# Affine part of two layer norms moved from the rows to the transposed rows and the residual

## Chip, cores and metric

One core of a Trainium2 chip runs the whole kernel. The metric is the device time of one execution in microseconds. The kernel before has a median of 3053.77 us over three runs (3049.5 to 3065.22).

## What is computed

A first block (two kinds of attention, a gate) is followed by two layers. Each layer has a mixer, then this (sequence and width are 1024, the feed-forward width is 4096):

```python
h = layer_norm(DN_ALPHA * h + mix, ln_mix_g[layer], ln_mix_b[layer])
h = layer_norm(DN_ALPHA * h + sq_relu_mlp(h, w_ff1[layer], w_ff2[layer]), ln_ffn_g[layer], ln_ffn_b[layer])
# layer_norm(x, g, b) = (x - mean) * rsqrt(var + eps) * g + b,  sq_relu_mlp(h, w1, w2) = square(relu(h @ w1)) @ w2
```

The change concerns the first of these two norms, in both layers. Its output `h` is used twice: as input of the first feed-forward map and as residual behind the second.

## The kernel before

Everything is in fp32, and a product is three matmuls on a high and a low part of each operand (a "split": ScalarE writes the high part, L155, and VectorE or GpSimd the low part, L157). Both feed-forward maps use a seven-product scheme on blocks of 512 (the products are numbered X[1] to X[7]).

**`lin_ln` (L1186)** is the last product of the mixer, then the norm. Eight tiles of 128 rows go through two column halves. In the second half each tile `t` goes through a chain: VectorE adds the residual (L1215), takes the statistics (L1143, L1144) and prepares the variance (L176), GpSimd raises it to -0.5 (L178), and VectorE applies `(z - mean) * g` (L1152) and `z * rs + b` (L1154), each on 128 x 1024, with `g` and `b` spread over all partitions in two pages that `ln_rows` loads (L1133). The result is stored for the residual (L1221, into `dzr`), and `to_T4` (L1171) turns each half of the row with four TensorE transposes (L1176) and one ScalarE copy of 128 x 512 out of PSUM (L1177) into a page `B`. From the pages `B`, VectorE builds differences (`op`, L1243), and splits make the blocks X[1] to X[7].

Four units of the first map (`ff1_unit`, L1279) begin inside `lin_ln`: the products X[1] and X[2] of units 0 to 3 are issued before the other blocks are ready. Each unit loads its weights (L1313, L1292, L1336), forms sums (L1293 to L1296), splits them, squares what comes out (L1310) and stores it (L1359, L1373).

**`ff` (L1450)** runs `ff1` and then the second map in four sweeps `k` of eight steps `j`. A step's operands are fetched two steps ahead (`AHEAD`, `ff2_ops`): four loads (L1408) and four splits on ScalarE and VectorE. The residual tiles `z` are read back from `dzr` (L1484), and `add` (L1475) adds a finished block of 4 tiles x 512 columns to them (L1479): the quarter (rows 0, columns 0) behind step (0,7), three quarters behind steps (1,7) and (2,7), the last behind sweep 3.

**What sets the order.** Each engine works its queue in order. The queues are laid out ahead of time by a planner from the order of the program and estimated durations, so a changed duration can change the order. All loads and stores of these stages are issued by SP, in order: an issue that waits for its page holds the later ones. Data lives in 48 pages of 128 x 1024 that are handed out first in, first out: a page taken is the one that was freed longest ago, and its new writer waits for the last reader of the old content. PSUM banks 2 and 3 take turns for the transposes.

Of the kernel before, what the change touches and what calls it, by code (L numbers as in the profile page):

```python
# [10 lines left out]
F32 = mybir.dt.float32  # L11
F32R = mybir.dt.float32r
I32 = mybir.dt.int32
AF = mybir.ActivationFunctionType
ALU = mybir.AluOpType
AX = mybir.AxisListType
MUL, ADD, SUB = ALU.mult, ALU.add, ALU.subtract
# [15 lines left out]
LN_EPS = 1e-5 * 4.0 ** -0.5  # L33
# [26 lines left out]
class Kern:  # L60
# [135 lines left out]
    def consts(self):  # L196
        nc, cp, i = self.nc, self.cp, self.i
        self.ident = cp.tile([128, 128], F32, name="ident")
        make_identity(nc, self.ident)
        self.ones = cp.tile([128, 128], F32, name="ones")  # L200
        nc.vector.memset(self.ones, 1.0)
        self.inv128 = cp.tile([128, 1], F32, name="inv128")
        nc.scalar.activation(self.inv128, self.ones[:, 0:1], AF.Copy, scale=1.0 / 128)
        self.halfpi = cp.tile([128, 1], F32, name="halfpi")
        nc.vector.memset(self.halfpi, float(np.float32(np.pi / 2)))
        self.nhalf = cp.tile([128, 64], F32, name="nhalf")
        nc.vector.memset(self.nhalf, -0.5)
        self.cols = cp.tile([128, 32], F32, name="cols")
        nc.sync.dma_start(self.cols, i["cols"])
        self.zeros = cp.tile([128, 128], F32, name="zeros")  # L210
        nc.gpsimd.memset(self.zeros, 0.0)
        self.gq8 = cp.tile([128, 2], F32, name="gq8")
        for j in range(2):
            nc.vector.tensor_scalar(self.gq8[:, j:j + 1], self.cols[:, 8 + 2 * j:9 + 2 * j], 0.125, None, MUL)
# [920 lines left out]
        return out  # L1135

    def ln(self, z, gb, eng=None, st=None):

        V = self.nc.vector
        mv, cs = self.sm(2, "mv"), (0,) if st is not None else (0, 1)  # L1140
        st = self.sm(12, "st") if st is None else st
        for c in cs:
            V.bn_stats(st[:, c * 6:c * 6 + 6], z[:, c * 512:(c + 1) * 512])  # L1143
        V.bn_aggr(mv, st.rearrange("p (n s) -> p n s", s=6))  # L1144
        rs = self.rsq(1, mv[:, 1:2], 1.0, LN_EPS)
        self.ln_apply(z, mv, rs, gb, np.s_[:], eng)

    def ln_apply(self, z, mv, rs, gb, cs, eng=None):

# [18 lines left out]
            nc.scalar.activation(h, src, AF.Copy)  # L1168
            nc.vector.tensor_tensor(l, src, h.bitcast(F32), SUB)

    def to_T4(self, src, dst):  # L1171

        nc = self.nc
        tp = self.bank("tr")
        for j in range(4):
            nc.tensor.transpose(tp[:, j * 128:(j + 1) * 128], src[:, j * 128:(j + 1) * 128], self.ident)  # L1176
        nc.scalar.activation(dst, tp.rearrange("p (c k) -> p c k", k=128), AF.Copy)  # L1177

    def split_T(self, src, X, p, pr, eng):

# [5 lines left out]
    def lin_ln(self, xp, wname, res, scale, j):  # L1186

        nc, i = self.nc, self.i  # L1190
        V, G = nc.vector, nc.gpsimd
        nat = lambda ch: [self.wload(i[wname][ch * 4 + k]).view("p (k f) -> p k f", k=2) for k in range(4)]
        ws = nat(0)
        z = [self.pg() for _ in range(8)]
        for t in range(8):
            nc.sync.dma_start(z[t].t, res[:, t, :])
        gb = self.ln_rows(j)
        x = self.tx(xp)
        self.dzr = self.dr([8, 128, 1024])
        X, B = {}, {}  # L1200
        units = deque()
        for ch in range(2):
            ws = ws if ch == 0 else nat(1)
            self.psum(**(dict(g1=[0, 1], tr=[2, 3], P=[4, 5, 0, 1], Q=[6, 7]) if ch else dict(g1=range(8))))
            for t in range(8):
                ps = self.bank("g1")
                hf, sl = t // 4, slice(t % 4 * 128, (t % 4 + 1) * 128)
                for kt in range(8):
                    w = [a[:, kt % 2, :] for a in ws[kt // 2]]
                    xh, xl = (a[:, sl] for a in x(kt, hf))  # L1210
                    self.mm(ps, xh, w[0], kt == 0, False)
                    self.mm(ps, xh, w[1], False, False)
                    self.mm(ps, xl, w[0], False, kt == 7)
                zs = z[t].t[:, ch * 512:(ch + 1) * 512]
                V.scalar_tensor_tensor(zs, ps, scale, zs, MUL, ADD)  # L1215
                if ch == 1:
                    if t % 4 == 3:
                        self.fr(*xp[0][hf], *xp[1][hf])
                    self.ln(z[t].t, gb)
                    self.dump(f"h{j}", [(np.s_[t::8, :], z[t].t)])  # L1220
                    nc.sync.dma_start(self.dzr[t], z[t].t)  # L1221
                    pr = t % 4 // 2
                    for K in range(2):
                        if t % 2 == 0:
                            B[K, hf, pr] = self.pg((128, 4, 256))
                        self.to_T4(z[t].t[:, K * 512:(K + 1) * 512], B[K, hf, pr].t[:, :, t % 2 * 128:(t % 2 + 1) * 128])
                    self.fr(z[t])
                    if hf == 0 and t % 2:
                        for K in range(2):
                            self.split_T(B[K, 0, pr].t, X, 1 + K, pr, V)  # L1230
                    if t in (4, 6):
                        units.append(self.ff1_unit(j, t // 2 - 2, X, True))
                        next(units[-1])
            self.fr(*(p for w in ws for p in w.pg))
        self.fr(*gb)
        b11, b12, b21, b22 = ([B[K, hf, pr] for pr in range(2)] for K in range(2) for hf in range(2))
        t2 = [self.pg((128, 4, 256)) for _ in range(2)]

        def op(p, o, x, y):

            for pr in range(2):
                if y is not None:
                    V.tensor_tensor(o[pr].t, x[pr].t, y[pr].t, SUB)  # L1243
            for pr in range(2):
                if p:
                    self.split_T(o[pr].t, X, p, pr, V)

        def first(k):

            for _ in range(2):  # L1250
                next(units[k])

        op(0, b11, b12, b11)
        op(6, t2, b22, b11)
        first(0)
        first(1)
        op(7, b12, b22, b12)
        self.fr(*b12)
        for k in (2, 3):
            units.append(self.ff1_unit(j, k, X, True))  # L1260
            next(units[k])
            first(k)
        next(units[0])
        op(5, b11, None, None)
        self.fr(*b11)
        op(4, b21, b21, t2)
        self.fr(*b21, *t2)
        op(3, b22, None, None)
        self.fr(*b22)
        return X, units  # L1270
# [179 lines left out]
    def ff(self, X, units, layer, last):  # L1450


        nc, i = self.nc, self.i
        V, A, G = nc.vector, nc.scalar, nc.gpsimd
        self.ff1(X, units, layer)
        z = [self.pg() for _ in range(8)]
# [5 lines left out]
        def fetch():  # L1462
            if steps:
                ahead.append(self.ff2_ops(layer, *steps.pop(0)))
# [17 lines left out]
            fetch()  # L1482
        for t in range(8):
            nc.sync.dma_start(z[t].t, self.dzr[t])  # L1484
        for k in range(3):
            for j in range(8):
                ops = ahead.popleft()
                fetch()
                if k == 1 and j == 0 and not last:
                    self.mla_tables()  # L1490
                for c, op in enumerate(ops):
                    for t in range(4):
                        mms(c, op, t, j == 0 and (k == 0 or k == 1 and c == 1), j == 7)
                    self.fr(*op[0], *op[1])
                    if j == 7:
                        for r, h in (((0, 0),), ((0, 1),), ((1, 1),))[k] if c == 0 else (((0, 0),), ((1, 1),), ((0, 1),))[k]:
                            add(c, r, h)

        gb = self.ln_rows(2 + layer)
# [33 lines left out]
        st = [self.sm(12, "sth") for _ in range(4)]  # L1533
        for t in range(4):
            V.bn_stats(st[t][:, 6:12], z[4 + t].t[:, 512:])
        if last:
            for t in range(4):
                for n, op in enumerate(tail):
                    mms(0, op, t, False, n == 3)
                zs = z[4 + t].t[:, :512]  # L1540
# [304 lines left out]
def layout(v):  # L1845
    o = {}
    f32 = np.float32
    v = {k: np.asarray(a) for k, a in v.items()}
# [4 lines left out]
        o["w_" + n] = w[:, :, c].reshape(4, 2, 128, 512).transpose(0, 2, 1, 3).reshape(4, 128, 1024)  # L1853
    wz = v["w_in"][0].reshape(8, 128, 8, 4, 128)[:, :, [3, 7]]
    o["w_z"] = wz.transpose(2, 3, 1, 0, 4).reshape(8, 128, 1024)
    cols = np.zeros((128, 32), f32)
    cols[:, 0:8] = v["norm_g"][0].reshape(8, 128).T
    for j, n in ((8, "q_norm_a"), (9, "k_norm_a"), (10, "q_norm_b"), (11, "k_norm_b")):
        cols[:, j] = np.tile(v[n][0], 2)
# [1 line left out]
    o["cols"] = cols  # L1861
    cols[:, 13:15] = v["kv_norm_g_2"].reshape(2, 128).T
    cols[:, 15:18] = v["q_norm_g_2"][0].reshape(3, 128).T
    o["lamv"] = np.broadcast_to(np.stack([v[n][0] for n in ("lam_q1", "lam_k1", "lam_q2", "lam_k2")])[None], (128, 4, 64))
    p_, j_ = np.arange(128)[:, None], np.arange(1920)[None]
    rel = j_ - 896 - p_
    n = np.abs(rel)
# [7 lines left out]
    c = cb * 16 + qc  # L1875
# [5 lines left out]
    for row in range(16):  # L1881
        rb, qr = row // 8, row % 8
        rs = min(max(row - 4, 0), 8)
# [8 lines left out]
    pr = lambda a: a.reshape(32, 2, 64, -1).transpose(1, 2, 0, 3).reshape(128, 32, -1)  # L1892
# [47 lines left out]
```

## Time and profile before

| | us |
|---|---|
| median of 3 runs | 3053.77 |
| profiled execution | 3052.07 |
| its span in the trace | 3050.3 |
| granted clock over the span | 0.982 |

The profile is of one execution; times inside it count from the start of its span. The engines are PE (TensorE), PEld (its weight loads), DVE (VectorE), ACT (ScalarE), POOL (GpSimd) and SP (which issues DMAs); a q behind a name is the engine's queue. In rows, `p` is a page, `ps` PSUM, `dr` a buffer in DRAM, `in_...` an input, and `out<-in` says what is written from what. The granted clock is given as a share of full speed. In the stage of layer 0 the tiles go through the norm from 1262 to 1323 us, in layer 1 from 2360 to 2421 us; the second map runs from 1637 and from 2730 us.

### The profile page before, as it was taken

How to read it: one execution, taken by the hardware profiler on the slowest of the kernel's cores; microseconds unless marked ns; L12 is line 12 of the kernel's file. 1: busy time of each engine (PE TensorE's matmuls, PEld its weight loads, DVE VectorE, ACT ScalarE, POOL GpSimd, SP SyncE). 2: the span in 40 equal slices, each digit the busy share in tenths (PEclk: the TensorE clock that was granted, in tenths of full speed). 3: DMA queues.
4: the chain of work that ended last, by engine and by line, in shares of the span. 5: the costliest groups of instructions: out<-in, count | busy, mean ns of one | idle time of the engine just before them, and what ended most of it. 6: DMA issues, size and time to landing. Idle time of an engine off the chain costs nothing.

```text
span 3050.3 us, 38397 instructions
## 1 busy us (share of the span) xinstructions
PE 2917.8 (96%) x14380; PEld 2403.1 (79%) x14380; DVE 1879.5 (62%) x2754; ACT 1188.6 (39%) x1810; POOL 1053.8 (35%) x694
## 2 busy tenths in 40 slices
PE   7999889998999899989999999999999999999998
PEld 6777667776777788867887888988898778878887
DVE  8555547765359700486667875655553966667666
ACT  4333237775324322142224433345563432334331
POOL 5545527754522333234441002112353244420001
PEclk9999999999999999999999999999999999999999
DMA  4353463368545113134448877311123334479673
GB/s 163 131 177 115 124 199 104 93 193 249 192 158 166 42 56 128 59 123 150 152 150 317 295 252 251 110 44 48 34 75 125 121 131 152 152 268 340 237 273 134
DMA packets 240923, 479.04 MB, mean 157 GB/s; under 512 B 26816, under 2 KB 76224, under 8 KB 240736
## 3 DMA queue, kind: packets, MB, share of 16 engines
q1 hardware_dynamic: 240592, 476.45, 46.2%
q8 instruction: 113, 1.85, 0.3%
q14 instruction: 74, 0.61, 0.1%
q10 hardware_dynamic: 144, 0.13, 0.0%
HBM read 320.00 MB, written 148.11 MB: 153 GB/s over the span
## 4 chain that ended last, share of the span: by engine, by line
PE 55%; DVE 10%; DMA 5%; issue 3%; POOL 2%; ACT 1%; SPq 0%; DVEq 0%; POOLq 0%; ACTq 0%
PE ps L170 23%; PE ps L1471 19%; PE ps L1276 10%; DMA p<-in_w_ff 3%; POOL p L157 1%; DMA p<-dr 1%; PE ps L1753 1%; DVE p L1030 1%; DVE p L157 1%; DVE p L1310 1%; DVE p L1043 1%; ACT p L155 1%; DMA dr<-p 1%; DVE p L1154 0%; DVE p L1036 0%
## 5 line engine op out<-in xcount | busy, mean ns | idle before, releaser
L170 PE MATMUL ps<-p,p 128*128 128x512 f32 (+6 forms) x7448 | 1532.1, 365 | 62.9 <-POOL p L157 11.7
L170 PEld LDWEIGHTS ps<-p,p 128*128 128x128 f32 (+2 forms) x7448 | 1214.5, 185 | 311.4 <-issue 50.3
L157 POOL TENSOR_TENSOR p<-p,p 128x1024 fp32r<-128x1024 f32 (+2 forms) x272 | 604.5, 2235 | 946.5 <-ACT p L155 861.2
L155 ACT ACTIVATE p<-p 128x1024 fp32r<-128x1024 f32 (+2 forms) x558 | 520.9, 959 | 959.0 <-DMA p<-in_w_ff 160.3
L1276 PE MATMUL ps<-p,p 128*128 128x512 f32 x2688 | 631.8, 396 | 31.8 <-ACT p L155 12.4
L1276 PEld LDWEIGHTS ps<-p,p 128*128 128x128 f32 x2688 | 509.2, 191 | 151.8 <-ACT p L155 14.7
L1471 PE MATMUL ps<-p,p 128*128 128x512 f32 x2688 | 613.0, 390 | 3.4 <-DVE p L1479 1.6
L1471 PEld LDWEIGHTS ps<-p,p 128*128 128x128 f32 x2688 | 503.6, 188 | 110.6 <-issue 2.4
L157 DVE TENSOR_TENSOR p<-p,p 128x1024 fp32r<-128x1024 f32 (+1 forms) x286 | 315.4, 1129 | 109.7 <-ACT p L155 108.6
L178 POOL TENSOR_TENSOR rsd<-rst,nhalf 128x1 f32<-128x1 f32 (+1 forms) x64 | 104.8, 1639 | 534.9 <-DVE rst L176 533.1
L1310 DVE SCALAR_TENSOR_TENSOR p<-p 128x512 f32<-128x512 f32 x96 | 116.6, 1214 | 2.2
L1122 DVE SCALAR_TENSOR_TENSOR p<-p,ps 128x1024 f32<-128x1024 f32 x8 | 9.8, 1221 | 141.4 <-ACT p L1121 141.4
L496 DVE CUSTOM_DVE_ANT_0 p<-ps,bw 128x1024 f32<-128x1024 f32 x64 | 77.3, 1219 | 30.7 <-PE ps L170 21.2
L498 ACT ACTIVATE p<-p,m 128x1024 f32<-128x1024 f32 x64 | 73.4, 1149 | 31.6 <-DVE m L496 19.6
L1295 DVE TENSOR_TENSOR p<-p,p 128x512 f32<-128x512 f32 x32 | 34.8, 1088 | 75.0 <-DMA p<-in_w_ff 75.0
L511 POOL TENSOR_TENSOR p<-p,p 128x1024 f32<-128x1024 f32 x32 | 76.8, 2405 | 2.0
L1747 POOL TENSOR_SCALAR p<-p,rz 128x256 f32<-128x256 f32 (+6 forms) x64 | 48.7, 762 | 68.7 <-DVE rz L1746 67.2
L1757 DVE TENSOR_TENSOR p<-ps,p 128x512 fp32r<-128x512 f32 (+3 forms) x96 | 50.9, 553 | 33.0 <-ACT p L1756 32.3
L1177 ACT ACTIVATE p<-ps 128x512 f32<-128x512 f32 x32 | 17.5, 594 | 129.5 <-PE ps L1176 129.4
L157 DVE TENSOR_TENSOR p<-ps,p 128x1024 fp32r<-128x1024 f32 (+1 forms) x42 | 42.0, 1015 | 39.9 <-ACT p L155 37.2
L510 POOL TENSOR_SCALAR p<-p,c 128x1024 f32<-128x1024 f32 x32 | 37.1, 1158 | 85.0 <-DVE c L509 62.1
L663 POOL TENSOR_SCALAR p<-p,rz 128x384 f32<-128x384 f32 x64 | 38.1, 601 | 68.3 <-DVE rz L662 53.3
(266 smaller groups left out, 2569.8 us busy)
## 6 DMA issues: line engine op xcount, KB each, us to landing
p<-dr SPq DMA_DIRECT2D x254, 512.0 KB
p<-in_w_ff SPq DMA_DIRECT2D x184, 512.0 KB
dr<-p SPq DMA_DIRECT2D x126, 512.0 KB
dr<-p SPq DMA_DIRECT2D x248, 256.0 KB
bw<-in_rpbw SPq DMA_DIRECT2D x16, 768.0 KB
dr<-p SPq DMA_DIRECT2D x80, 128.0 KB
p<-p SPq DMA_DIRECT2D x64, 128.0 KB
p<-dr SPq DMA_DIRECT2D x32, 256.0 KB
```

The source lines that it names most:

```text
L155: nc.scalar.activation(hi, src, AF.Copy, scale=scale)
L157: (eng or nc.gpsimd).tensor_tensor(lo, src, hi.bitcast(F32), SUB)
L170: self.nc.tensor.matmul(out, l, r, start=start, stop=stop)
L178: nc.gpsimd.tensor_tensor(dst, t, self.nhalf[:, :n], ALU.pow)
L496: V.tensor_tensor_reduce(out=s.t, in0=ps, in1=bw[:, 896 - 128 * t:1920 - 128 * t], scale=-1.0, scalar=3e38, op0=ADD, op1=ALU.min, accum_ou ...
L498: A.activation(s.t, s.t, AF.Exp, bias=m[:, c:c + 1], scale=-1.0, accum_out=z[:, c:c + 1])
L511: G.tensor_tensor(p[0].t, p[0].t, p[1].t, ADD)
L1276: self.nc.tensor.matmul(ps, w[a][:, kt, :], x[b][kt // 2].t[:, kt % 2, :], start=start and kt == 0 and (a, b) == (0, 0), stop=kt == 3 and ...
L1310: V.scalar_tensor_tensor(h, h, 0.0, h, ALU.max, MUL)
L1471: nc.tensor.matmul(ps[c][t], a[x].t[:, kt, t * 128:(t + 1) * 128], b[y].t[:, kt, :], start=start and kt == 0 and (x, y) == (0, 0), stop=st ...
L1747: G.tensor_scalar(s.t[:, :n], s.t[:, :n], rz, 1.0, MUL, MUL)
L1757: V.tensor_tensor(atl[kq][:, :nb, qi * 128:(qi + 1) * 128], tv, oh.bitcast(F32), SUB)
```

## The change

The norm in `lin_ln` now only makes `(z - mean) * rs`, in one VectorE instruction on 128 x 1024. This is what is stored in `dzr` and transposed. After the transposition a feature is a partition, so `g` and `b` are one value per partition; four ScalarE instructions of 128 x 128 with a scale and a bias per partition replace the one copy of 128 x 512 per half row. `g` and `b` for this lie in 32 further columns of the constant `cols`. The residual gets its scale and bias in `ff`: `ln_rows` is called there behind the residual's loads, its two pages live until step (1,5), and VectorE multiplies and adds each quarter of `z` in steps (0,3), (1,1), (1,3) and (1,5), 8 instructions of 128 x 512 each time.

```diff
-        self.cols = cp.tile([128, 32], F32, name="cols")
+        self.cols = cp.tile([128, 64], F32, name="cols")
...
     def ln(self, z, gb, eng=None, st=None):
+        mv, rs = self.ln_stats(z, st)
+        self.ln_apply(z, mv, rs, gb, np.s_[:], eng)
+
+    def ln_stats(self, z, st=None):
...
-        rs = self.rsq(1, mv[:, 1:2], 1.0, LN_EPS)
-        self.ln_apply(z, mv, rs, gb, np.s_[:], eng)
+        return mv, self.rsq(1, mv[:, 1:2], 1.0, LN_EPS)
...
-    def to_T4(self, src, dst):
+    def to_T4(self, src, dst, gb):
...
-        nc.scalar.activation(dst, tp.rearrange("p (c k) -> p c k", k=128), AF.Copy)
+        for j in range(4):
+            nc.scalar.activation(dst[:, j], tp[:, j * 128:(j + 1) * 128], AF.Identity, bias=gb[:, 1, j:j + 1], scale=gb[:, 0, j:j + 1])
...
-        gb = self.ln_rows(j)
+        gb = self.cols[:, 32 + 16 * j:48 + 16 * j].rearrange("p (c k) -> p c k", c=2)
...
-                    self.ln(z[t].t, gb)
-                    self.dump(f"h{j}", [(np.s_[t::8, :], z[t].t)])
+                    mv, rs = self.ln_stats(z[t].t)
+                    V.tensor_scalar(z[t].t, z[t].t, mv[:, 0:1], rs, SUB, MUL)
...
-        self.fr(*gb)
...
         for t in range(8):
             nc.sync.dma_start(z[t].t, self.dzr[t])
+        gz = self.ln_rows(layer)
+
+        def affine(r, h):
+
+            c = slice(h * 512, (h + 1) * 512)
+            for t in range(4):
+                zs = z[4 * r + t].t[:, c]
+                V.tensor_tensor(zs, zs, gz[0].t[:, c], MUL)
+                V.tensor_tensor(zs, zs, gz[1].t[:, c], ADD)
+
...
+                if (k, j) in ((0, 3), (1, 1), (1, 3), (1, 5)):
+                    affine(*((0, 0), (0, 1), (1, 1), (1, 0))[0 if k == 0 else 1 + j // 2])
+                if (k, j) == (1, 5):
+                    self.fr(*gz)
```

## Rows read from the trace of the kernel before

**Rows 1.** Busy time, share of the span, instructions (the page, part 1)

```profile
PE 2917.8 (96%) x14380; PEld 2403.1 (79%) x14380; DVE 1879.5 (62%) x2754; ACT 1188.6 (39%) x1810; POOL 1053.8 (35%) x694
```

**Rows 2.** Busy us by stretch: PE, PEld, DVE, ACT, POOL, clock, DMA share

```profile
1270.00:1335.00 65.00, 57.11 (x275) 46.11 (x274) 59.73 (x76) 26.91 (x45) 21.53 (x12) 0.95 0.38 134
1335.00:1340.00 5.00, 5.00 (x15) 3.95 (x14) 5.00 (x7) 2.89 (x6) 0.00 (x0) 0.59 0.00 0
1365.00:1370.00 5.00, 5.00 (x24) 4.14 (x23) 2.49 (x4) 1.72 (x3) 3.14 (x2) 1.00 0.84 295
2430.00:2435.00 5.00, 3.84 (x8) 2.75 (x9) 4.92 (x6) 3.54 (x7) 0.00 (x0) 0.50 0.14 54
2435.00:2440.00 5.00, 5.00 (x17) 3.91 (x17) 5.00 (x8) 2.00 (x4) 0.00 (x0) 0.68 0.01 3
```

**Rows 3.** Waits of PE: 1150 to 1345 us, then 2310 to 2480 (total us, times, longest)

```profile
PE ps L1276 <- ACT p L155: 6.4, 2, 4.1
PE ps L1276 <- DVE p L157: 1.2, 2, 0.9
PE ps L1276 <- DVE p L1330: 0.3, 1, 0.3
...
PE ps L1276 <- ACT p L155: 5.8, 2, 3.5
PE ps L1276 <- DVE p L157: 1.4, 2, 1.2
```

**Rows 4.** Timeline of layer 0: start, us, engine, instruction [idle before <-releaser]

```profile
1290.98 1.28 DVE L1152 SCALAR_TENSOR_TENSOR p<-p,mv,p 128x1024 f32<-128x1024 f32 x1
1291.20 1.46 POOL L178 TENSOR_TENSOR rsd<-rst,nhalf 128x1 f32<-128x1 f32 x1 [1.53 <-DVE rst L176]
1292.70 1.28 DVE L1154 SCALAR_TENSOR_TENSOR p<-p,rsd,p 128x1024 f32<-128x1024 f32 x1 [0.45 <-POOL rsd L178]
```

**Rows 5.** By line and form: count, busy us, mean ns, idle before

```profile
L1154 DVE SCALAR_TENSOR_TENSOR p<-p,rsd,p 128x1024 f32<-128x1024 f32 x31 | 39.3, 1276 | 5.3 <-POOL rsd L178 5.3
...
L1294 DVE TENSOR_TENSOR p<-p,p 128x512 f32<-128x512 f32 x32 | 21.8, 680 | 12.0 <-DMA p<-in_w_ff 12.0
...
L864 DVE TENSOR_SCALAR p<-p 128x1024 f32<-128x1024 f32 x4 | 2.8, 691 | 0.1
...
L376 ACT ACTIVATE p<-ps,rx 128x512 f32<-128x512 f32 x40 | 27.4, 685 | 82.6 <-PE ps L170 82.6
...
L1177 ACT ACTIVATE p<-ps 128x512 f32<-128x512 f32 x32 | 17.5, 594 | 129.5 <-PE ps L1176 129.4
...
L350 ACT ACT_TABLE_LOAD x4 | 5.1, 1283 | 0.1
...
L1756 ACT ACTIVATE p<-ps 128x128 fp32r<-128x128 f32 x16 | 4.4, 277 | 0.5 <-PE ps L1753 0.4
```

**Rows 6.** Timeline at the end of the stage of layer 0

```profile
1325.54 1.06 ACT L155 ACTIVATE p<-p 128x1024 fp32r<-128x1024 f32 x1 [0.51 <-DMA dr<-p]
...
1326.65 1.49 PE L1276 MATMUL ps<-p,p 128*128 128x512 f32 x4 [2.31 <-ACT p L155]
```

**Rows 7.** Waits of ScalarE, 1282 to 1346 us

```profile
ACT p L155 <- DVE p L1243: 7.8, 3, 4.9
```

**Rows 8.** Chain of waits, stage of layer 1

```profile
2424.96 5.09 DMA p<-in_w_ff
```

**Rows 9.** Second map of layer 0, by stretch (columns as in rows 2)

```profile
1645.00:1650.00 5.00, 5.00 (x24) 4.14 (x23) 5.00 (x7) 2.96 (x4) 0.00 (x0) 1.00 1.05 402
1700.00:1750.00 50.00, 50.00 (x222) 41.40 (x221) 44.09 (x50) 18.79 (x19) 0.00 (x0) 1.00 0.83 292
```

**Rows 10.** Timeline of VectorE in the second map of layer 0

```profile
1777.50 1.21 DVE L1438 TENSOR_TENSOR p<-p,p 128x1024 f32<-128x1024 f32 x1
...
1814.16 0.68 DVE L1479 SCALAR_TENSOR_TENSOR p<-ps,p 128x512 f32<-128x512 f32 x1
```

**Rows 11.** Timeline of PE, second map of layer 1

```profile
2745.16 35.12 PE L1471 MATMUL ps<-p,p 128*128 128x512 f32 x152 [0.77 <-ACT p L155]
```

## What the change will do to the time: the prediction

> **What bounds the kernel now.** I read the page first. TensorE is busy for 96% of the span, VectorE for 62% [rows 1]: what the change can give must come out of the few places where TensorE stands still, and only if VectorE is what it waits for there. So next I read the stretches around the changed norm. In 1270 to 1335 us VectorE is busy for 59.73 of 65 us and TensorE for 57.11, while ScalarE has 26.91 [rows 2]: this is one of the places where VectorE is the full engine. The waits of TensorE price it. In the stage of layer 0 it waits 6.4 + 1.2 + 0.3 = 7.9 us, in layer 1 5.8 + 1.4 = 7.2 us [rows 3], and nearly all of it falls behind the last tile, when VectorE has to finish norm, differences and splits at once. Those waits cost more than themselves: right behind them the granted clock is 0.59 in layer 0 and 0.50 (the lower of its two levels, 1.2 GHz) and 0.68 in layer 1, and 15, 8 and 17 matmuls pass in 5 us where a stretch at clock 1.00 has 24 [rows 2]. At 5/24 = 0.21 us each, layer 0 loses 9 x 0.21 = 1.9 us. Layer 1 has 25 matmuls in 10 us, of which 1.16 were waiting: 8.84/0.21 = 42, so 17 are missing, 3.6 us. All that the stage can give back is therefore 7.9 + 7.2 + 1.9 + 3.6 = 20.6 us, 0.7% of the time.
>
> **The sum's base.** The profiled execution took 3052.07 us (span 3050.3, 1.8 around it), 1.7 under the median of 3053.77. The three runs shown lie 0.5% apart, which is about what a measurement of this kernel can tell from no change: 15.3 us, so under 3038.5 counts as faster and over 3069.0 as slower.
>
> **Norm on VectorE.** Each tile loses two instructions of 1.28 us [rows 4, 5] and gains one with a single tensor source. The trace has no such instruction with two values per partition. Its nearest row is the 128x1024 TENSOR_SCALAR at 691 ns, and the upper bound is the 1276 ns of the one it replaces [rows 5]. I take 0.69, the same shape and operation: 2 x 1.276 - 0.69 = 1.86 us less VectorE work a tile, 14.9 us a layer.
>
> How much of this reaches TensorE is the main choice. The first three tiles pass while TensorE has products to do, so only tiles 3 to 7 count. In the old order GpSimd's power (1.46 us) runs beside the first of the two instructions (1.28 us), and the second waited 0.45 us for it [rows 4]. The new instruction needs mean and power both, so VectorE has nothing of this tile to do in those 1.46 us. The tile's own chain from the start of the power shrinks only from 1293.98 - 1291.20 = 2.78 us to 1.46 + 0.04 + 0.69 = 2.2 us, by 0.6 us. Lower bound per layer: 0.6 us for the tiles before and the full 1.86 us for the last, whose instructions stand in a stretch without idle time: 2.5 us. Upper bound: five tiles at 1.86 = 9.3 us, cut to the 7.9 and 7.2 us that there are. I take the last tile in full and half of tiles 4 to 6, on the view that splits or statistics of other tiles are put into every second gap: 1.86 + 0.5 x 3 x 1.86 = 4.65 us a layer, **-9.3 us**. What is late next is the difference for X[7] (L1243) and the lower part of unit 3's weights.
>
> **Clock.** TensorE will still wait some 3 us a layer, and the clock fell behind waits of 2.3 and 4.1 us [rows 3, 6]. Bounds 0 and 5.5 us; I take 1 us a layer, **-2 us**.
>
> **ScalarE.** A 128x128 copy out of PSUM takes 277 ns, and a value per partition adds 685 - 594 = 91 ns [rows 5]. A piece with scale and bias is then 277 + 182 = 459 ns, four of them 1.84 us against 0.594, at most 1.25 us more a half row, 2.5 us a tile, 20 us a layer. ScalarE has that room (26.91 + 20 of 65 us). On the path it costs only where a split stands behind these pieces. In that stretch ScalarE waits 7.8 us for VectorE's differences [rows 7], which covers most of the 3 x 2.5 = 7.5 us of tiles 5 to 7; if the cover were gone, 7.5 us a layer. Against it, the split at 1325.54 waited for a store of the last tile, whose page it was to fill, and TensorE 2.31 us for that split [rows 6]. The norm no longer takes two pages here, every later writer gets a page freed two places earlier, and this one goes to a page that TensorE has left. I take +0.5 us a layer, **+1 us**.
>
> Identity occurs nowhere in the trace. If it asked for a table load of 1.28 us [rows 5] before and after, twice a layer, that is at most 5.1 us; I take 0 and leave the bound to the range. The Trainium skill ("ScalarE: Activation LUTs", section "Table sets: the hidden batching unit") says that cheap functions, identity among them, are part of every set, so that no load would come; no run here shows it, and by it the sum stays as it is.
>
> **Second map, VectorE.** Four quarters of 8 instructions of 0.68 us [rows 5] are 21.8 us a layer. They lie in sweeps 0 and 1, where TensorE has no gap to speak of and VectorE is busy for up to 44.09 of 50 us [rows 9]. The cover is the distance by which it works ahead: it starts on sweep 2 (L1438) at 1777.50, while the first block of sweep 1 is added only at 1814.16, 36.7 us later [rows 10]. The 3 x 5.4 = 16.3 us in sweep 1 leave 20 us of it. Cost 0; without that cover each quarter would cost up to 5.4 us.
>
> **Second map, loads.** `ln_rows` leaves SP's queue ahead of the norm, where TensorE is not waiting, and its two issues and two pages come between the residual's loads and those of step 2. They are 2 x 0.52 MB in the stretch where the DMA engines are full, 402 GB/s at share 1.05 [rows 9]: 1.05 MB / 402 GB/s = 2.6 us for the loads queued behind, those of steps 2 and 3. Step 1 had no slack (TensorE waited 0.77 us in it [rows 11]); from then on the distance grows by some us a step. Bounds: 0 if step 1's loads go first, as the order of the program has it, and 2.6 us if the rows go first. I take 0.7 us a layer, **+1.4 us**. If an issue waits for its page, SP holds the fetches behind it, and step 2 is late next. The transposes, the store into `dzr` and the 32 more columns of a constant change nothing that I can price.
>
> **Sum.** -9.3 - 2 + 1 + 1.4 = -8.9 us: 3052.07 - 8.9 = **3043.2 us**.
>
> **Rivals.**
> *The whole wait goes (20%).* The order of VectorE's queue is planned anew, and if it fills every gap behind a power, the stage's upper bound holds: 20.6 us less, 1.4 us for the loads back, 3032.9 us. For it: VectorE is the full engine of the stage [rows 2]. Against it: the difference for the last tile still needs power, transposes and eight ScalarE pieces in a row.
> *The loads decide (12%).* In layer 1 the chain runs through a weight load of 5.09 us [rows 8] whose issue stands behind a store on SP. If the next wait is for such loads, VectorE idles instead and the stage gives about 1 us a layer, less 0.7: 3051.5 us. This is the case in which the change does not do what it says.
> *ScalarE is late (10%), slower than before.* If the planner leaves the splits behind the pieces of tiles 5 to 7, each layer pays 7.5 us and gets only the lower bound of 2.5 us back: 2 x 5 = 10 us, 3062 us. It decides from the point where the pieces in front of the last splits exceed the 7.8 us that ScalarE waits there now [rows 7]; 7.5 is just under it, which speaks for and against. The Trainium skill ("ScalarE: Activation LUTs", section "Rules for kernel authors") gives multiply and add to VectorE and not to ScalarE; by that rule this rival is how it goes. In busy time the trace agrees, with up to 2.5 us added a tile against 1.86 taken away.
>
> **Chances and range.** My case has 58%, and its own bounds run from 3036 (gain 7.5 a layer, loads free) to 3052 (lower bound of the gain, 2.6 us a layer for the loads, no clock). Faster by over 0.5% is most of the first rival and the quick end of my case: 0.28. Slower by over 0.5% needs the third rival together with full costs of loads and tables (3062 + 2.6 x 2 + 5.1): 0.07. The rest, 0.65, is within 0.5%. The range 3030 to 3060 leaves out the far end of the first rival and most of the third.
>
> **What would show it.** Right: in the norm one TENSOR_SCALAR of about 0.7 us a tile, idle before it put down to the power, TensorE's waits in the two stages down from 7.9 and 7.2 us to about 3, those around a clock of 0.5 shorter, and no longer wait in the second map. Wrong: new waits of TensorE for ScalarE's Identity pieces or splits, the new instruction near 1.3 us, a wait in step 1 or 2 of the second map grown by over 1 us, or a table load in the stage. A change of several us in the stages between, through other pages and orders, would also make the total wrong without touching these steps.

## The result, and the profile after

The changed kernel takes 3078.66 us, median of 5 runs (3076.87 to 3080.91); the kernel before, on the same chip, 3056.32 (3049.5 to 3065.22). The ratio is 1.0073, 95% interval 1.0058 to 1.0088: **slower by 0.7%**, outside the predicted range, on the side that had been given a chance of 7%. The profiled executions have spans of 3050.3 and 3076.3 us, 26.0 apart.

Where they went is read from the starts of fixed matmuls in the two traces (the lines of the matmuls are now L1280 for the first map, L1475 for the second). The first row of the table runs from a fixed matmul ahead of the norm to the 169th matmul of the first map, the second from there to the first matmul of the second map; both together are "norm and first map" further down:

| us | before, layer 0 / 1 | after, layer 0 / 1 | difference of both |
|---|---|---|---|
| norm, up to the 169th matmul of the first map | 130.8 / 138.0 | 128.1 / 133.9 | -6.8 |
| rest of the first map | 278.3 / 273.9 | 275.7 / 276.3 | -0.1 |
| second map, sweep 0 (384 matmuls) | 91.1 / 91.2 | 106.7 / 106.8 | **+31.2** |
| everything else | | | +1.7 |

The last line holds +2.9 us in the first 1230 us, whose instructions the change does not touch; over the programs below that part lay between -3.0 and +9.4 us of before. The kernels are therefore compared stage by stage.

The first part of the page (busy time, share of the span, instructions) hardly shows a change against [rows 1]:

```profile
PE 2924.6 (95%) x14380; PEld 2410.7 (78%) x14380; DVE 1872.6 (61%) x2802; ACT 1220.1 (40%) x1906; POOL 1056.2 (34%) x694
```

By line and form (count, busy us, mean ns, idle before), the new instructions and the table loads:

```profile
L1181 ACT ACTIVATE p<-ps,cols 128x128 f32<-128x128 f32 x128 | 47.6, 464 | 112.3 <-PE ps L1179 112.2
...
L350 ACT ACT_TABLE_LOAD x4 | 5.1, 1283 | 0.1
...
L1224 DVE TENSOR_SCALAR p<-p,mv,rsd 128x1024 f32<-128x1024 f32 x16 | 13.0, 810 | 4.2 <-POOL rsd L178 3.8
```

The prices are near those of the prediction: 464 ns a piece (459 foreseen), 810 ns for the norm's one instruction (690 taken, 0.12 us a tile too little), and still only the four table loads of [rows 5]. So the places decide, not the prices. TensorE's waits (total us, times, longest) in the norm of layer 0 (1150 to 1345 us), the norm of layer 1 (2330 to 2480), and the second map of layer 0 (1640 to 2000); the last line is the only one of that last stretch in the kernel before:

```profile
PE ps L1280 <- ACT p L155: 3.3, 2, 2.3
PE ps L1280 <- DVE p L157: 2.2, 1, 2.2
PE ps L1280 <- DVE p L1334: 0.6, 1, 0.6
...
PE ps L1280 <- ACT p L155: 4.6, 3, 2.3
PE ps L1280 <- DVE p L157: 2.2, 1, 2.2
PE ps L1280 <- DVE p L1334: 1.6, 1, 1.6
...
PE ps L1475 <- ACT p L155: 7.1, 1, 7.1
PE ps L1475 <- DVE p L157: 5.4, 1, 5.4
...
PE ps L1471 <- DVE p L157: 1.0, 1, 1.0
```

In the norm 7.9 us became 6.1 in layer 0 [rows 3]. In layer 1 they did not fall: they are 8.4 us, and were 8.1 up to the 169th matmul (the 7.2 us of the prediction are the two largest lines of that view). What layer 1 gained, 4.1 us, came with the clock, as the windows from the fixed matmul to the 169th show, first before, then after (total, PE, PEld, DVE, ACT, POOL, granted clock, DMA share, GB/s):

```profile
2318.77:2456.76 137.99, 129.79 (x592) 105.78 (x590) 96.16 (x125) 42.96 (x69) 40.04 (x19) 0.95 0.30 103
...
2333.59:2467.50 133.91, 125.58 (x585) 102.78 (x583) 80.38 (x117) 57.20 (x117) 39.67 (x19) 0.97 0.31 110
```

How far that carries, the six kernels below whose norm is that of the changed kernel show. Up to the 169th matmul they take 127.0 to 128.2 us in layer 0 and 134.4 to 138.3 in layer 1: there the changed kernel's 133.9 is the shortest, and rows_only and late_rows, with a clock of 0.95, gain nothing. So layer 0's 2.7 us stand, and layer 1's 4.1 us lie inside what the same instructions vary by.

The new thing stands in the two lines of L1475: 12.5 us in a place where TensorE had waited 1.0. The timeline of that place (start, us, engine, instruction, count), first TensorE, then VectorE, then SP's queue:

```profile
1638.26 10.13 PE L1475 MATMUL ps<-p,p 128*128 128x512 f32 x44
1655.53 4.92 PE L1475 MATMUL ps<-p,p 128*128 128x512 f32 x12 [7.14 <-ACT p L155]
1665.87 34.35 PE L1475 MATMUL ps<-p,p 128*128 128x512 f32 x142 [5.42 <-DVE p L157]
...
1639.79 2.35 DVE L157 TENSOR_TENSOR p<-p,p 128x1024 fp32r<-128x1024 f32 x2
1642.06 0.68 DVE L1372 TENSOR_TENSOR p<-p,p 128x512 f32<-128x512 f32 x1
1642.66 7.30 DVE L1496 TENSOR_TENSOR p<-p,p 128x512 f32<-128x512 f32 x12
...
1661.59 0.68 DVE L1375 TENSOR_TENSOR p<-p,p 128x512 f32<-128x512 f32 x1
1662.19 2.49 DVE L1497 TENSOR_TENSOR p<-p,p 128x512 f32<-128x512 f32 x4
...
1680.17 0.68 DVE L1497 TENSOR_TENSOR p<-p,p 128x512 f32<-128x512 f32 x1
...
1632.11 0.33 SPq L1133 DMA_DIRECT2D p<-in_ln  x1
...
1636.01 0.34 SPq L1133 DMA_DIRECT2D p<-in_ln  x1
1637.28 0.37 SPq L1412 DMA_DIRECT2D p<-in_w_ff  x1
...
1651.73 10.88 SPq L1377 DMA_DIRECT2D dr<-p  x3
1662.72 2.02 SPq L1412 DMA_DIRECT2D p<-dr  x2
```

L1496 and L1497 are the multiplies and adds of the residual. The program has them at steps (0,3), (1,1), (1,3) and (1,5); VectorE's queue has **all 32 in one clump** between 1642.66 and 1680.85 us, from the first step on, and the splits (L157) of the next steps between them and behind them. The loads of the two rows (L1133) went out before a weight load (L1412) of the first steps. And a store (L1377) whose values VectorE makes in L1372 to L1375 sits at the head of SP's queue: VectorE reaches L1375 only at 1661.59, the three stores take from 1651.73 to 1662.61, and every load behind them waits. The windows of this stretch (columns as above) show the rest of the price:

```profile
1650.00:1655.00 5.00, 0.00 (x0) 0.00 (x0) 5.00 (x7) 1.52 (x2) 0.00 (x0) 0.78 1.06 399
1655.00:1660.00 5.00, 4.47 (x11) 3.55 (x12) 5.00 (x8) 2.37 (x3) 0.00 (x0) 0.54 0.51 199
1660.00:1665.00 5.00, 0.45 (x2) 0.01 (x1) 5.00 (x8) 2.00 (x2) 0.00 (x0) 0.80 0.36 118
1665.00:1670.00 5.00, 4.13 (x10) 3.26 (x11) 5.00 (x6) 2.01 (x2) 0.00 (x0) 0.51 0.75 251
1670.00:1675.00 5.00, 5.00 (x24) 4.11 (x23) 5.00 (x7) 0.10 (x1) 0.00 (x0) 1.00 0.01 3
```

In the stretch VectorE has not one idle moment, the DMA engines fall from share 1.06 to 0.36 although weights are wanted, and behind each wait the granted clock is near 0.5, the 1.2 GHz level, so that 11 and 10 matmuls pass in 4.47 and 4.13 busy us where 5 us at 1.00 have 24. The waits are 12.5 of sweep 0's 15.6 us, the low clock most of the rest. Layer 1 shows the same: waits of 7.1 and 5.3 us, and 15.6 us in sweep 0.

### The profile page after: what moved, and what is told of

Its sections match the earlier page's. It is cut to its first block, busy times and chain, and to the rows that moved or that the text cites. A ratio compares the mean times of both kernels' runs of the same rounds, so it can differ in the third digit from the quotient of the medians.

```text
span 3076.3 us, 38539 instructions
## 1 busy us (share of the span) xinstructions
PE 2924.6 (95%) x14380; PEld 2410.7 (78%) x14380; DVE 1872.6 (61%) x2802; ACT 1220.1 (40%) x1906; POOL 1056.2 (34%) x694
## 4 chain that ended last, share of the span: by engine, by line
PE 74%; DVE 13%; DMA 6%; issue 3%; ACT 2%; POOL 1%; SPq 0%; DVEq 0%; ACTq 0%; POOLq 0%
PE ps L170 38%; PE ps L1475 19%; PE ps L1280 14%; DMA p<-in_w_ff 2%; DMA dr<-p 2%; DVE p L157 1%; POOL p L157 1%; DVE p L1030 1%; PE ps L1771 1%; PE ps L666 1%; DVE p L1043 1%; DVE p L496 1%; DMA p<-dr 1%; ACT p L155 1%; PE ps L519 1%
## 5 line engine op out<-in xcount | busy, mean ns | idle before, releaser
L157 POOL TENSOR_TENSOR p<-p,p 128x1024 fp32r<-128x1024 f32 (+2 forms) x272 | 616.7, 2280 | 953.1 <-ACT p L155 849.4
L155 ACT ACTIVATE p<-p 128x1024 fp32r<-128x1024 f32 (+2 forms) x558 | 520.8, 962 | 954.4 <-DMA p<-dr 189.5
L1280 PE MATMUL ps<-p,p 128*128 128x512 f32 x2688 | 627.9, 395 | 30.3 <-ACT p L1345 8.9
L1475 PE MATMUL ps<-p,p 128*128 128x512 f32 x2688 | 619.8, 393 | 25.0 <-ACT p L155 14.3
L1280 PEld LDWEIGHTS ps<-p,p 128*128 128x128 f32 x2688 | 509.2, 190 | 146.0 <-ACT p L155 10.8
L1475 PEld LDWEIGHTS ps<-p,p 128*128 128x128 f32 x2688 | 509.6, 190 | 133.1 <-ACT p L155 15.1
L157 DVE TENSOR_TENSOR p<-p,p 128x1024 fp32r<-128x1024 f32 (+1 forms) x286 | 317.8, 1133 | 109.5 <-ACT p L155 108.2
L178 POOL TENSOR_TENSOR rsd<-rst,nhalf 128x1 f32<-128x1 f32 (+1 forms) x64 | 93.1, 1456 | 558.8 <-DVE rst L176 556.9
L1314 DVE SCALAR_TENSOR_TENSOR p<-p 128x512 f32<-128x512 f32 x96 | 108.5, 1131 | 2.3
L1181 ACT ACTIVATE p<-ps,cols 128x128 f32<-128x128 f32 x128 | 47.6, 464 | 112.3 <-PE ps L1179 112.2
L498 ACT ACTIVATE p<-p,m 128x1024 f32<-128x1024 f32 x64 | 73.4, 1148 | 30.7 <-DVE m L496 19.4
L157 DVE TENSOR_TENSOR p<-ps,p 128x1024 fp32r<-128x1024 f32 (+1 forms) x42 | 42.1, 1014 | 37.1 <-ACT p L155 34.2
L1219 DVE SCALAR_TENSOR_TENSOR p<-ps,p 128x512 f32<-128x512 f32 x32 | 21.7, 687 | 70.2 <-PE ps L170 70.2
```

What stands on the lines that cost most here:

```text
L155: nc.scalar.activation(hi, src, AF.Copy, scale=scale)
L157: (eng or nc.gpsimd).tensor_tensor(lo, src, hi.bitcast(F32), SUB)
L178: nc.gpsimd.tensor_tensor(dst, t, self.nhalf[:, :n], ALU.pow)
L498: A.activation(s.t, s.t, AF.Exp, bias=m[:, c:c + 1], scale=-1.0, accum_out=z[:, c:c + 1])
L1280: self.nc.tensor.matmul(ps, w[a][:, kt, :], x[b][kt // 2].t[:, kt % 2, :], start=start and kt == 0 and (a, b) == (0, 0), stop=kt == 3 and ...
L1314: V.scalar_tensor_tensor(h, h, 0.0, h, ALU.max, MUL)
```

## The experiments

Sweep 0 of the second map and the whole time of each kernel; where the runs allow it, with the ratio to the kernel before:

| kernel | sweep 0, layer 0 / 1 | norm and first map, layer 0 / 1 | us (runs) | ratio, 95% interval |
|---|---|---|---|---|
| before | 91.1 / 91.2 | 409.1 / 411.8 | | |
| changed | 106.7 / 106.8 | 403.9 / 410.2 | 3078.66 (5) | 1.0073 [1.0058, 1.0088] |
| norm_only | 91.2 / 91.2 | 405.7 / 412.7 | 3055.34 (10) | 1.0006 [0.9995, 1.0017] |
| rows_only | 97.1 / 97.0 | 408.3 / 414.8 | 3061.15 (1) | |
| late_rows | 100.1 / 99.1 | 405.3 / 413.0 | 3074.06 (1) | |
| quarter_rows | 91.2 / 91.2 | 404.0 / 408.7 | 3044.45 (9) | 0.9969 [0.9957, 0.9981] |
| one_copy | 91.4 / 91.1 | 403.4 / 405.6 | 3043.03 (4) | 0.9952 [0.9935, 0.9970] |
| two_passes | 91.2 / 91.5 | 411.0 / 411.5 | 3056.52 (10) | 1.0001 [0.9992, 1.0011] |
| rows_late_only | 90.7 / 91.3 | 407.2 / 406.9 | 3044.31 (1) | |
| pool_affine | 115.6 / 117.6 | 404.7 / 409.6 | 3104.94 (1) | |

The kernels from norm_only to quarter_rows ran beside runs of the kernel before at 3055.09 us (18 runs), those from one_copy to pool_affine beside runs at 3057.55 (13). The stages are read from one trace of each kernel.

**norm_only: the norm's part of the change alone.**

```diff
-        gz = self.ln_rows(layer)
-        def affine(r, h):
...
-                if (k, j) in ((0, 3), (1, 1), (1, 3), (1, 5)):
-                    affine(*((0, 0), (0, 1), (1, 1), (1, 0))[0 if k == 0 else 1 + j // 2])
-                if (k, j) == (1, 5):
-                    self.fr(*gz)
```

> The residual's scale and bias and the loads of their rows are left out; norm and transposes stay as in the changed kernel. Theory (the 32 residual instructions of a layer, all laid at the start of sweep 0 by the planner, hold up VectorE's splits there): sweep 0 takes 91 us again instead of 107 in both layers, the total is about 31 us under the changed kernel, near 3048 us. Rival 1 (the two row loads in the stretch where the DMA engines are full): the same. Rival 2 (ScalarE's pieces make the norm stage and what follows late): sweep 0 is not the place, the total stays over 3070 us.

Sweep 0 is back at 91.2 us in both layers, so all of the 15.6 us hang on the residual's part. The total is 23 us under the changed kernel, though, and not 31: it is that of before, so the norm alone bought nothing that can be measured. Its two halves are taken apart by two_passes and one_copy.

**rows_only: the rows are loaded and their pages held, without the arithmetic.**

```diff
-        def affine(r, h):
...
-                if (k, j) in ((0, 3), (1, 1), (1, 3), (1, 5)):
-                    affine(*((0, 0), (0, 1), (1, 1), (1, 0))[0 if k == 0 else 1 + j // 2])
```

> As norm_only, but the two rows are loaded where the changed kernel loads them and their pages are held until step (1,5); only the 32 VectorE instructions a layer are left out. Theory: sweep 0 takes 91 to 94 us, the loads alone cost at most 2.6 us a layer. Rival 1: sweep 0 stays at 105 us or more.

97.1 and 97.0: the loads and their held pages alone cost 5.9 us a layer, more than twice the upper bound that had been set. The timeline of TensorE and ScalarE, then of SP's queue:

```profile
1651.82 48.43 PE L1475 MATMUL ps<-p,p 128*128 128x512 f32 x203 [4.87 <-ACT p L155]
1648.82 2.95 ACT L155 ACTIVATE p<-p 128x1024 fp32r<-128x1024 f32 x3 [3.72 <-DVE p L157]
...
1629.12 0.33 SPq L1133 DMA_DIRECT2D p<-in_ln  x1
...
1633.00 0.34 SPq L1133 DMA_DIRECT2D p<-in_ln  x1
1634.32 0.37 SPq L1412 DMA_DIRECT2D p<-in_w_ff  x1
```

The rows stand ahead of a weight load of the first steps. TensorE waits 4.87 us where it waited 0.92 in quarter_rows, 3.95 more. The windows of rows_only (columns as above) give the rest:

```profile
1650.00:1655.00 5.00, 3.18 (x8) 2.51 (x9) 4.93 (x5) 3.84 (x4) 0.00 (x0) 0.50 1.05 404
1655.00:1660.00 5.00, 5.00 (x21) 4.06 (x20) 4.30 (x4) 1.10 (x2) 0.00 (x0) 0.86 1.04 413
```

8 matmuls in 3.18 us at clock 0.50, where 0.21 us each makes 15, and 21 instead of 24: some 10 x 0.21 = 2.1 us. 3.95 + 2.1 = 6.0.

Which part of the loads does it is not shown. The splits behind which TensorE waited stood themselves for 3.72 us, and what ended that, by the profile, was not a load but VectorE's splits, which suggests a page that came free late. The two pages held, the bytes and the places in SP's queue are not taken apart by any run.

**late_rows: the rows loaded at (0,3), the first quarter at (0,5).**

```diff
-        gz = self.ln_rows(layer)
...
-                if (k, j) in ((0, 3), (1, 1), (1, 3), (1, 5)):
...
+                if (k, j) == (0, 3):
+                    gz = self.ln_rows(layer)
+                if (k, j) in ((0, 5), (1, 1), (1, 3), (1, 5)):
...
```

> Everything as in the changed kernel, but the rows are loaded in step (0,3) and the first quarter is done in step (0,5). Theory: the 32 instructions now stand behind the splits of steps 0 to 4, where VectorE is 15 us and more ahead of TensorE, and their 22 us take up most of that: sweep 0 takes 91 to 95 us, total 3050 to 3058 us. Rival 1: also near 91 us, since the loads come behind the full stretch. If VectorE's work in itself were too much wherever it stands, sweeps 0 and 1 together would still be 15 us longer than before.

A miss: 100.1 and 99.1 us. The timeline (VectorE, TensorE, SP) says why:

```profile
1672.97 9.11 DVE L1495 TENSOR_TENSOR p<-p,p 128x512 f32<-128x512 f32 x15
...
1705.58 2.08 PE L1475 MATMUL ps<-p,p 128*128 128x512 f32 x4 [4.33 <-ACT p L155]
...
1675.93 10.21 SPq L1412 DMA_DIRECT2D p<-in_w_ff  x4
```

The clump only moved: as soon as the rows were there, all 32 instructions stood in VectorE's queue again (L1495 x15 in a row), ahead of splits and between them. Four weight loads took SP 10.21 us to issue beside it, and TensorE stood still for 4.33 us before 1705.58.

**quarter_rows: each quarter loads its own half rows at its step.**

```diff
-        gz = self.ln_rows(layer)
...
+            p = self.pg((128, 2, 512))
+            nc.sync.dma_start(p.t, i["ln"][layer, :, c][None].to_broadcast([128, 2, 512]))
             for t in range(4):
                 zs = z[4 * r + t].t[:, c]
-                V.tensor_tensor(zs, zs, gz[0].t[:, c], MUL)
-                V.tensor_tensor(zs, zs, gz[1].t[:, c], ADD)
+                V.tensor_tensor(zs, zs, p.t[:, 0], MUL)
+                V.tensor_tensor(zs, zs, p.t[:, 1], ADD)
+            self.fr(p)
...
-                if (k, j) == (1, 5):
-                    self.fr(*gz)
```

> Each quarter of the residual loads its own half rows into one page, at the step where the program does the quarter, so that no quarter can be planned earlier: four loads of 0.5 MB a layer instead of two. Theory: 8 instructions at a time find cover, sweep 0 takes 91 to 93 us and sweep 1 87 us as before, total near 3049 us, 30 us under the changed kernel. Rival 1: twice the loads, so at least as long as the changed kernel where they fall into the full stretch, sweep 0 over 100 us.

Sweep 0 takes 91.2 us again, with twice the bytes of rows in four loads. On VectorE's timeline the quarters now stand apart:

```profile
1663.23 2.49 DVE L1497 TENSOR_TENSOR p<-p,p 128x512 f32<-128x512 f32 x4
1665.64 1.29 DVE L1498 TENSOR_TENSOR p<-p,p 128x512 f32<-128x512 f32 x2
...
1730.01 2.48 DVE L1497 TENSOR_TENSOR p<-p,p 128x512 f32<-128x512 f32 x4
```

The same 32 instructions cost nothing when they are spread. This version **beats both kernels**: 3044.45 us, 0.3% under the kernel before by the ratio, 1.1% under the changed one.

**rows_late_only: late_rows without its arithmetic.**

```diff
-        gz = self.ln_rows(layer)
...
-        def affine(r, h):
...
-                if (k, j) in ((0, 3), (1, 1), (1, 3), (1, 5)):
-                    affine(*((0, 0), (0, 1), (1, 1), (1, 0))[0 if k == 0 else 1 + j // 2])
+                if (k, j) == (0, 3):
+                    gz = self.ln_rows(layer)
```

> The two rows are loaded at step (0,3) and their pages held to step (1,5) as in late_rows, but nothing is multiplied or added to the residual, which so lacks its scale and bias. Sweep 0 was 100.1 and 99.1 us in late_rows, 97.1 and 97.0 with the rows loaded at the start and no arithmetic, 91.2 without either. Theory, the 32 instructions in one clump ahead of the splits cost late_rows its 8 to 9 us, and the loads cost only by standing ahead of step 1's: sweep 0 is 91.2 to 92.5 us in both layers. Rival, the 1 MB of loads and the two held pages cost wherever they stand: 95 to 97.

90.7 and 91.3 us: nothing is lost, as the theory had it. This and late_rows differ in the 32 instructions alone: the clump costs 9.4 and 7.8 us there, and the same loads and pages are free once step 1 has its weights. Beside rows_only against the changed kernel (106.7 - 97.1 = 9.6 and 106.8 - 97.0 = 9.8) that is the second measurement of the same price.

**pool_affine: the changed kernel with the residual's arithmetic on GpSimd.**

```diff
-                V.tensor_tensor(zs, zs, gz[0].t[:, c], MUL)
-                V.tensor_tensor(zs, zs, gz[1].t[:, c], ADD)
+                G.tensor_tensor(zs, zs, gz[0].t[:, c], MUL)
+                G.tensor_tensor(zs, zs, gz[1].t[:, c], ADD)
```

> The changed kernel with the residual's 32 multiplies and adds on GpSimd, which does little in the second map; they may stand in one clump there, as they did on VectorE. Sweep 0 was 106.7 us in both layers of the changed kernel, 97.1 and 97.0 with the loads alone. Theory, what costs the last 9.6 us is that the instructions stand in VectorE's queue ahead of the splits of steps 1 to 5: sweep 0 falls to 96 to 98 us. Rival, VectorE is slowed by GpSimd's traffic, so that the splits come late all the same: VectorE's 128x1024 splits are longer than their 1.2 us and sweep 0 stays over 100.

The rival held: 115.6 and 117.6 us. The forms in 1630 to 1780 us:

```profile
L1497 POOL TENSOR_TENSOR p<-p,p 128x512 f32<-128x512 f32 x16 | 35.8, 2270 | 0.0
...
L157 DVE TENSOR_TENSOR p<-p,p 128x1024 fp32r<-128x1024 f32 x52 | 84.8, 1658 | 11.2 <-ACT p L155 10.1 <-PE ps L1475 0.9
```

and the timeline of VectorE and TensorE:

```profile
1665.39 2.32 DVE L157 TENSOR_TENSOR p<-p,p 128x1024 fp32r<-128x1024 f32 x1 [1.12 <-ACT p L155]
1667.74 2.20 DVE L1430 TENSOR_TENSOR p<-p,p 128x1024 f32<-128x1024 f32 x1
...
1667.30 3.78 PE L1475 MATMUL ps<-p,p 128*128 128x512 f32 x8 [15.65 <-ACT p L155]
```

GpSimd takes 2270 ns an add where VectorE takes 680, and VectorE's splits take 1658 ns in the mean (1218 in the changed kernel). VectorE's queue is free of the clump here, and the splits are late all the same, so this run says nothing for or against the queue. The pair of late_rows and rows_late_only does.

**two_passes and one_copy: what the norm's two halves are worth.** Both keep quarter_rows' second map. two_passes gives VectorE its second pass back, with a page of ones and a page of zeros:

```diff
+        oz = [self.pg() for _ in range(2)]
+        for c in range(2):
+            nc.gpsimd.memset(oz[c].t, 1.0 - c)
...
-                    V.tensor_scalar(z[t].t, z[t].t, mv[:, 0:1], rs, SUB, MUL)
+                    V.scalar_tensor_tensor(z[t].t, z[t].t, mv[:, 0:1], oz[0].t, SUB, MUL)
+                    V.scalar_tensor_tensor(z[t].t, z[t].t, rs, oz[1].t, MUL, ADD)
```

> As quarter_rows, but VectorE again does two passes of 128x1024 on each normalized row (with a page of ones and a page of zeros), as the kernel before did, in front of ScalarE's four pieces. Theory A, VectorE's chain behind each row sets when the last row can be transposed: the stage is longer by the 1.87 us of one row (2 x 1.28 less 0.69) up to the 4.65 us that the forecast took, so 405.9 to 408.7 us in layer 0 and 410.6 to 413.4 in layer 1. Rival, the passes are hidden by the products of the other rows and the gain comes from another place: 404.0 and 408.7, within 0.5 us.

one_copy takes ScalarE's four pieces away, so that the input of the first map lacks its scale and bias:

```diff
-        for j in range(4):
-            nc.scalar.activation(dst[:, j], tp[:, j * 128:(j + 1) * 128], AF.Identity, bias=gb[:, 1, j:j + 1], scale=gb[:, 0, j:j + 1])
+        nc.scalar.activation(dst, tp.rearrange("p (c k) -> p c k", k=128), AF.Copy)
```

> The residual is treated as in quarter_rows; the transposed rows go through ScalarE's single Copy of 128x512, so the scale and bias of the maps' input are left out. Stage of norm and first map, from a fixed matmul ahead of the norm to the first matmul of the second map: quarter_rows 404.0 us in layer 0 and 408.7 in layer 1 (before 409.1 and 411.8). Theory A, the four pieces (4 x 464 ns against 680 ns, 1.2 us a transposition) stand on the path behind the last row and eat part of the norm's gain: the stage is 1.2 to 2.4 us shorter in each layer, 401.6 to 402.8 and 406.3 to 407.5. Rival, the pieces lie beside TensorE's work and the evictions of the first map's units set the end: both stages within 0.5 us of quarter_rows. Sweep 0 of the second map stays at 91 to 92 us.

Before, two_passes, quarter_rows and one_copy are the four corners of a square. The time up to the first map's 169th matmul, TensorE's waits (in 1150 to 1345 us for layer 0, from the fixed matmul to the 169th for layer 1), and the mean granted clock between these two matmuls:

| | layer 0 / 1 | waits, layer 0 / 1 | clock, layer 0 / 1 |
|---|---|---|---|
| two passes, one copy (before) | 130.8 / 138.0 | 7.9 / 8.1 | 0.96 / 0.95 |
| two passes, four pieces (two_passes) | 132.5 / 141.5 | 9.9 / 9.1 | 0.95 / 0.94 |
| one pass, four pieces (quarter_rows) | 127.8 / 135.4 | 6.6 / 8.8 | 0.97 / 0.97 |
| one pass, one copy (one_copy) | 123.0 / 129.5 | 2.4 / 5.0 | 0.99 / 1.00 |

With the pieces in place, the second pass is worth 4.7 and 6.1 us; with the single copy, 7.8 and 8.5, of which the waits themselves are 5.5 and 3.1 and the clock the rest. The pieces cost 1.7 and 3.5 us behind two passes, 4.8 and 5.9 behind one. One trace stands for each corner, and the same norm alone varied by 1.2 us in layer 0 and by 4.4 in layer 1 among the kernels above: layer 0's 4.7, 7.8 and 4.8 are clear of that, its 1.7 and most of layer 1's figures are not. Over the whole stage, for which the expectations were written, the pieces show 0.6 and 3.1 us and the second pass 6.9 and 2.8: all but the last lie outside what either theory gave. The queues are planned anew in each kernel, and the rest of the first map takes from 270.0 to 280.6 us in these kernels. Where the pieces cost is seen on ScalarE's timeline behind the last transposes, in quarter_rows:

```profile
1328.12 2.90 ACT L1181 ACTIVATE p<-ps,cols 128x128 f32<-128x128 f32 x8 [5.69 <-PE ps L1179]
1330.88 0.63 ACT L1330 ACTIVATE p<-ps 128x512 f32<-128x512 f32 x1
1331.36 5.34 ACT L155 ACTIVATE p<-p 128x512 fp32r<-128x512 f32 x10
```

and in one_copy:

```profile
1327.74 1.09 ACT L1180 ACTIVATE p<-ps 128x512 f32<-128x512 f32 x2 [4.60 <-PE ps L1179]
1328.89 0.60 ACT L1329 ACTIVATE p<-ps 128x512 f32<-128x512 f32 x1
1329.38 0.62 ACT L155 ACTIVATE p<-p 128x512 fp32r<-128x512 f32 x1
```

The splits that TensorE waits for (L155) stand behind the last row's pieces: they begin 3.24 us after the start of those in quarter_rows and 1.64 us in one_copy. That is 1.6 of layer 0's 4.8 us; where the pieces cost the others was not followed up.

## Why the prediction was wrong

**The step that failed is "Second map, VectorE".** It says of the four quarters: "They lie in sweeps 0 and 1", and prices them against the distance by which VectorE works ahead in sweep 2, "Cost 0; without that cover each quarter would cost up to 5.4 us". It read their place from the program. The trace has all of them in the first steps, where the next step of the same prediction had found "no slack", and they cost 9.6 and 9.8 us, together 19.4. The material for this was at hand: the queues are laid out by a planner that may change the order, which the prediction allowed for in the norm (two rivals rest on it) and not here. Their inputs, the residual and the two rows, are there early, and nothing else in the program holds them back. Shown is that the clump follows the arrival of the rows (changed kernel, late_rows) and is gone where each quarter's rows come at its step (quarter_rows); by which rule the planner picks was not looked into.

**"Second map, loads" was mis-sized**, 0.7 us a layer with an upper end of 2.6 "if the rows go first". They did go first, and it was 5.9 and 5.8 us: TensorE's wait grew by 3.95 us in layer 0, and the clock behind it took 2.1 more, a term that the prediction had for the norm's waits and left out here.

**"Norm on VectorE" and "Clock" came out near their sum, but not by their terms.** With the four pieces in place, two_passes against quarter_rows gives 4.7 + 6.1 = 10.8 us against 9.3 + 2. But the waits fell only by 3.3 us in layer 0 and 0.3 in layer 1, 3.6 where 9.3 stood; the other 7.2 us came with the clock (0.95 to 0.97 and 0.94 to 0.97), where 2 stood. That the two errors cancel is luck, and layer 1's part is not far above what the same norm varies by. In the changed kernel itself the waits of 6.1 and 8.4 us are far from the "about 3" that was to show the step right; there the clock over layer 0's stage stayed at 0.96, and layer 1's rose from 0.95 to 0.97 without a shorter wait.

**"ScalarE" was mis-sized**: the 464 ns of a piece were foreseen (459), the place was not. The +0.5 us a layer rested on ScalarE's idle time in front of splits [rows 7]; up to the first map's 169th matmul it was 4.8 and 5.9 us by quarter_rows against one_copy. That is the mechanism of the third rival, at about two thirds of its price in layer 0 and four fifths in layer 1. It did not decide the sign: with it and without the second map's costs, quarter_rows is faster than before.

**The rest.** No table load came, as the page "ScalarE: Activation LUTs" of the Trainium skill has it (section "Table sets: the hidden batching unit"): the four of before are the four of after. The Trainium skill's rule that multiply and add belong to VectorE (the same page, section "Rules for kernel authors"), which it grounds on bf16, fits the square in fp32: four pieces on ScalarE took back more than half of what VectorE's lost pass gave. The measured terms, -6.8 up to the 169th matmul, -0.1 in the rest of the first map, +11.7 for the loads, +19.4 for the clump and +1.7 elsewhere, come to 25.9 of the 26.0 us between the profiled executions; the last of them is what was left over, so that the sum proves nothing by itself. The predicted 3043.2 us is close to what quarter_rows takes, but by other terms than the sum had: less from the norm (5.5 us up to the 169th matmul), and some from stages that no step named (2.7 in the rest of the first map).

**Left open:** why stages with the same instructions differ by several us from program to program (the first 1230 us, the norm of layer 1, the rest of the first map). The planner is the nearest cause; no run isolates it. Open too is what in the two loads cost 5.9 us, their bytes, their places in SP's queue or their pages.

## What to carry to other kernels

Where queues are laid out by a planner, the place of an instruction in the program is no promise: work that is off the path and ready early can be pulled in front of work that is on it. Hold it back by its data, as with a load at its own step, and read the engine's timeline at the first moment at which the inputs are there. Price a wait with the clock that falls behind it, and an added load by what it stands ahead of: the same two rows cost 5.9 us in front of step 1's weights and nothing three steps later.

## What the runs showed of the hardware

GpSimd's multiplies and adds slowed VectorE's two-input instructions while both ran: the 128x1024 split, 1.22 us by itself, took 2.3 us beside them, a 128x1024 difference 2.2 (the timeline of pool_affine above). GpSimd itself needed 2.1 to 2.3 us for each 128x512 instruction that VectorE does in 0.68, and that takes GpSimd 1.29 us at another place of the kernel before:

```profile
L594 POOL TENSOR_TENSOR p<-p,p 128x512 f32<-128x512 f32 x8 | 10.3, 1293 | 7.8 <-DVE p L593 4.1 <-DVE rz L662 2.1 <-DVE rz L507 1.6
```

The page "SBUF — State Buffer" of the Trainium skill (section "SBUF: two separate sides") has the two engines share one pair of ports that one instruction holds to its end, for VectorE those with two inputs in SBUF among them where GpSimd's instruction reads SBUF; the trace agrees, with the durations of both up while both run. And VectorE's TENSOR_SCALAR with two values per partition took 810 ns for 128x1024, where the one of the same shape without them took 691 [rows 5].
